# Up projection of a hybrid decoder layer: seven products for eight (Strassen-Winograd), gated activations kept in DRAM, one down projection over all 22 channel tiles

## The chip, the cores and the metric

The kernel runs on one core of a Trainium2 chip. The metric is the device time of one execution in microseconds (us). The kernel before takes 1457.86 us (median of 3 runs, 1457.52 to 1457.88). The changed kernel is to be compared with it on the same chip.

The engines are named as in the profile: PE (TensorE, matmuls and transposes), PEld (the loads of the stationary operand, which lie beside PE), DVE (VectorE), ACT (ScalarE), POOL (GpSimd) and SP (SyncE, which here only issues DMAs).

## The reference, cut to what matters

One layer, 1024 tokens of width 1024, float32:

```python
u = rms_norm(h) @ w_in
oA = gated_delta_net(u[...])          # 4 heads
oB = diff_attention(u[...])           # 4 heads
h = h + concat(oA, oB) @ w_out
g, v = split(causal_dwconv3(rms_norm(h) @ w_up))   # 2 x 2816 channels, 3 taps and a bias
h = h + (silu(g) * v) @ w_down
```

The change touches only the last two lines and the second norm ahead of them (and where one set of buffers of `w_out` lies).

## The kernel before

**Arithmetic.** Every large matmul is done in three: an operand is split into a high part (an ACT copy, L196) and the remainder (a subtraction on DVE, L200, or POOL, L198), and hi·hi, hi·lo and lo·hi are summed in PSUM. A matmul has a stationary operand of 128x128 and a moving one of 128x512.

**Attention and output projection.** After delta rule and attention, `wout_b` goes through eight blocks of 128 tokens, from the last to the first: transposes of the mixed heads (`trm`), the product with the second half of `w_out` (`pwo`, two halves of 512 columns), residual, second norm (`u2`), and eight transposes (`tr`), which `split_T` turns into the high and low parts of the normed activations `x2n`, channels on partitions (ACT L251, DVE L252).

**Up projection.** `ffn_up(j)` makes channel tile j of the gate and tile 22+j of the other half. Each is [128 channels, 1024 tokens] in PSUM: `gemm_T` (matmuls L416, L417, L418) runs over 8 row blocks of `w_up`, 3 matmuls each, for both halves of 512 tokens: 48 matmuls a tile, 96 for a pair, 22 pairs. Tile j's weight is one load of 128 columns (512 KB) and one split of 1024 elements. The convolution over tokens reads PSUM: an ACT Identity with the last tap and the bias (L1169), two fused multiply-adds on DVE (L1172), then Silu on ACT (L1175) for the gate, and the product of the two on POOL (L1177).

**Down projection.** The products stay in SBUF, twelve tiles in the first run of `ffn_down`, ten in the second, since there is room for no more. Each run splits them (L1199 on ACT, L1200 on DVE), multiplies by `w_down` (`mm3`, L377 to L379, eight PSUM banks at once, one for each token block, for one half of the 1024 output columns at a time), adds the residual (L1222) and writes to DRAM: the first run to `h2_dram`, the second, which reads `h2_dram` as its residual, to the output.

**What sets the order.** A tile framework schedules each engine's instructions by priorities (the table `PRI`) and by the order of the code, and puts semaphores between them. Buffers come from rings: `g` (16 of 128x1024), `w` (5, split weights), `raw` (3, weights as loaded), `c` (4), `l` (2), `j` (2), `xn` (4 of 128x4096, the normed activations). A new tile takes the slot of an old one of its ring and waits for the last reader of that. SP's queue issues DMAs in order, and one that waits for a slot holds those behind it. In `before` the first pair's matmuls stand between those of `wout_b`'s last blocks, since they need the later half of the tokens alone.

## Time and profile before

| | |
|---|---|
| median of 3 runs | 1457.86 us |
| profiled execution, span from first to last instruction | 1450.8 us |
| mean granted TensorE clock | 0.988 of full |
| PE busy | 1382.0 us (95%), 8191 matmuls |
| DVE, ACT, POOL busy | 753.7, 530.8, 255.4 us (52%, 37%, 18%) |
| DMA | 128.9 MB |

The profiled execution's own time lies in its span; the median of the runs is 7.06 us above the span. A row of the slices below gives the busy tenths of 40 stretches of 36.3 us. PE has 9s from the 21st slice (about 725 us) to the 39th: that is the feed-forward part, with the up and down projections, and DVE, ACT and POOL have 3s, 2s and 0s or 1s there.

```text
PE   7988898989979999999999999999999999999998
DVE  6457978885343477867753333333333333333343
ACT  6435454532333456574332222222221222222221
POOL 3144312140342253430001011010000011010000
```

In the groups of instructions "mean ns of one" of a matmul is the time of one from start to modelled end, and matmuls overlap; how often one can start is read from the number that start in a window in which PE was never idle.

### The profile page before, as it was taken

Reading aid. Unit: us, or ns where it says so; the run is one execution under the profiler, and the core shown is the slowest. Engines: PE = TensorE matmul, PEld = TensorE weight load, DVE = VectorE, ACT = ScalarE, POOL = GpSimd, SP = SyncE. Lnnn points to the kernel's source line nnn. Section 1 sums busy time; section 2 is a strip of 40 time slices with the busy share of each in tenths; the row PEclk is TensorE's granted clock in tenths of the full one; section 3 lists DMA queues with packets and bytes.
Section 4 is the critical chain, followed back from the end, with each engine's and each line's share of the span. In section 5 each row is a group of like instructions: output and inputs, shape, how many; then the busy total and the mean of one; then the engine's idle time right before and its main releaser. Section 6 shows DMA issues by size and latency. Waiting matters only on the chain.

```text
span 1450.8 us, 20362 instructions
## 1 busy us (share of the span) xinstructions
PE 1382.0 (95%) x8191; PEld 1166.8 (80%) x8191; DVE 753.7 (52%) x1579; ACT 530.8 (37%) x970; POOL 255.4 (18%) x199
## 2 busy tenths in 40 slices
PE   7988898989979999999999999999999999999998
PEld 7877677878979977777788888888888888888887
DVE  6457978885343477867753333333333333333343
ACT  6435454532333456574332222222221222222221
POOL 3144312140342253430001011010000011010000
PEclk8999999999999999999999999999999999999999
DMA  7321112121732467554321111113234111112231
GB/s 226 85 72 44 31 30 73 59 75 59 206 100 88 117 165 176 130 166 151 127 74 58 44 45 57 44 45 116 76 98 136 53 44 59 44 44 81 79 116 58
DMA packets 136221, 128.90 MB, mean 89 GB/s; under 512 B 8255, under 2 KB 111295, under 8 KB 136127
## 3 DMA queue, kind: packets, MB, share of 16 engines
q1 hardware_dynamic: 123647, 117.92, 26.1%
q0 software_dynamic: 11008, 8.39, 3.1%
q10 hardware_dynamic: 1472, 1.29, 0.3%
q8 instruction: 64, 1.05, 0.3%
q14 instruction: 30, 0.25, 0.1%
HBM read 92.44 MB, written 30.95 MB: 85 GB/s over the span
## 4 chain that ended last, share of the span: by engine, by line
PE 75%; DVE 11%; issue 5%; POOL 3%; ACT 3%; DMA 3%; SPq 0%; DVEq 0%; ACTq 0%; POOLq 0%
PE gT L418 12%; PE gT L417 12%; PE gT L416 12%; PE pd L377 6%; PE pd L379 6%; PE pd L378 5%; PE pn L397 4%; PE pn L398 3%; PE pn L400 3%; DVE acc L567 2%; PE pT L872 1%; DMA raw<-in_w_in_dram 1%; PE pwo L377 1%; PE pwo L379 1%; PE pao L930 1%
## 5 line engine op out<-in xcount | busy, mean ns | idle before, releaser
L416 PE MATMUL gT<-xn,whi 128*128 128x512 f32 x896 | 352.4, 393 | 0.8 <-ACT pT L427 0.8
L418 PE MATMUL gT<-xn,wlo 128*128 128x512 f32 x896 | 352.8, 394 | 0.0
L417 PE MATMUL gT<-xn,whi 128*128 128x512 f32 x896 | 351.8, 393 | 0.0
L200 DVE TENSOR_TENSOR wlo<-raw,whi 128x1024 fp32r<-128x1024 f32 x66 | 80.9, 1225 | 331.6 <-PE gT L417 266.5
L416 PEld LDWEIGHTS gT<-xn,whi 128*128 128x128 f32 x896 | 168.8, 188 | 34.7 <-ACT pT L427 1.2
L417 PEld LDWEIGHTS gT<-xn,whi 128*128 128x128 f32 x896 | 168.8, 188 | 34.0
L418 PEld LDWEIGHTS gT<-xn,wlo 128*128 128x128 f32 x896 | 169.0, 189 | 33.7
L1177 POOL TENSOR_TENSOR facc<-facc,facc 128x1024 f32<-128x1024 f32 x22 | 52.6, 2392 | 647.0 <-DVE facc L1172 608.2
L1169 ACT ACTIVATE facc<-gT,fcw 128x1024 f32<-128x1024 f32 x44 | 53.3, 1211 | 291.7 <-PE gT L418 291.7
L377 PE MATMUL pd<-whi,gh 128*128 128x512 f32 x352 | 137.5, 391 | 0.0
L378 PE MATMUL pd<-wlo,gh 128*128 128x512 f32 x352 | 137.0, 389 | 0.0
L379 PE MATMUL pd<-whi,gl 128*128 128x512 f32 x352 | 136.8, 390 | 0.0
L196 ACT ACTIVATE whi<-raw 128x1024 fp32r<-128x1024 f32 x100 | 105.1, 1051 | 48.9 <-PE pd L379 28.0
L1172 DVE SCALAR_TENSOR_TENSOR facc<-gT,fcw,facc 128x1023 f32<-128x1023 f32 x88 | 112.9, 1282 | 11.6 <-ACT facc L1169 10.1
L198 POOL TENSOR_TENSOR wlo<-raw,whi 128x1024 fp32r<-128x1024 f32 x34 | 83.7, 2471 | 191.4 <-PE gT L418 66.7
L397 PE MATMUL pn<-whi,xn 128*128 128x256 f32 x448 | 114.8, 290 | 0.0
L398 PE MATMUL pn<-whi,xn 128*128 128x256 f32 x448 | 114.2, 289 | 0.0
L1199 ACT ACTIVATE gh<-facc 128x1024 fp32r<-128x1024 f32 x40 | 42.5, 1061 | 159.8 <-PE pd L378 125.5
L1200 DVE TENSOR_TENSOR gl<-facc,gh 128x1024 fp32r<-128x1024 f32 x40 | 48.9, 1223 | 91.0 <-ACT gh L1199 91.0
L397 PEld LDWEIGHTS pn<-whi,xn 128*128 128x128 f32 x448 | 86.0, 192 | 0.4
L398 PEld LDWEIGHTS pn<-whi,xn 128*128 128x128 f32 x448 | 85.9, 192 | 0.1
L377 PEld LDWEIGHTS pd<-whi,gh 128*128 128x128 f32 x352 | 66.1, 188 | 15.1 <-ACT gh L1199 1.0
(304 smaller groups left out, 2219.6 us busy)
## 6 DMA issues: line engine op xcount, KB each, us to landing
raw<-in_w_up_dram SPq DMA_DIRECT2D x44, 512.0 KB, 3.8
raw<-in_w_down_dram SPq DMA_DIRECT2D x22, 512.0 KB, 3.8
raw<-in_w_in_dram SPq DMA_DIRECT2D x18, 512.0 KB, 4.0
pn_dram<-pn SPq DMA_DIRECT2D x16, 512.0 KB, 3.5
fres<-h_dram SPq DMA_DIRECT2D x16, 512.0 KB, 4.9
raw<-in_w_in_dram SPq DMA_DIRECT2D x17, 256.0 KB, 3.7
x<-in_x_dram SPq DMA_DIRECT2D x8, 512.0 KB, 5.8
qk<-pn_dram SPq DMA_DIRECT2D x8, 512.0 KB, 3.5
```

The costliest lines, as they stand in the source:

```text
L196: S.activation(hi, raw[:, 0:w], AF.Copy)
L198: G.tensor_tensor(lo, raw[:, 0:w], hi.bitcast(F32), op=ALU.subtract)
L200: V.tensor_tensor(lo, raw[:, 0:w], hi.bitcast(F32), op=ALU.subtract)
L377: PE.matmul(ps, lh, rh, start=first, stop=False)
L378: PE.matmul(ps, lh, rl, start=False, stop=False)
L379: PE.matmul(ps, ll, rh, start=False, stop=last)
L397: PE.matmul(o, xs(xn, 0, kt, a, b), wh, start=kt == 0, stop=False)
L398: PE.matmul(o, xs(xn, 1, kt, a, b), wh, start=False, stop=False)
L416: PE.matmul(o, whi[:, kt, :], xs(x_, 0, kt, *qs), start=kt == 0, stop=False)
L417: PE.matmul(o, whi[:, kt, :], xs(x_, 1, kt, *qs), start=False, stop=False)
L418: PE.matmul(o, wlo[:, kt, :], xs(x_, 0, kt, *qs), start=False, stop=kt == NK - 1)
L1172: V.scalar_tensor_tensor(acc[:, sft:], ps[:, :T - sft], fcw[:, jj * 44 + ct:jj * 44 + ct + 1], acc[:, sft:], op0=ALU.mult, op1=ALU.add)
```

## The change

The gate tile j and the up tile 22+j are taken together as a matrix product of 2x2 blocks: the weight rows in two halves of four row blocks, the two channel tiles, the tokens in two halves of 512. Seven products of 12 matmuls (4 row blocks by 3) replace eight. The sums that this takes:

- On the activations, in `combine` instead of `split_T`, token block by token block: T1, T2, T3, T4 are sums of the first and second halves of tokens and channels. The token halves "11", "21", "22" and T2 are split at once; T1, T3 and T4 are kept as sums and split by `mv_split` at the start of the feed-forward part (24 ACT, 16 DVE and 8 POOL instructions of 128x256).
- On the weights, for each j: four sums of 128x512 on POOL (L1269 to L1272), and splits of three tiles of 1024 and one of 512 where there were two of 1024.
- On the results, for each j: six DVE adds of 128x512 from PSUM to SBUF (L1280) and two ACT copies (L1288, L1297). The convolution (L1307, L1310) then reads SBUF.

`up_early` does the two products that need the later half of the tokens alone, for j = 0 and 1, before the transposes of the last token blocks. The eight PSUM banks become tiles of 512. `up` writes each product of gate and up tile to `act_dram`; `down` runs once over 22 tiles, loads them back (for both column halves, 42 loads in all, since the last pair is kept), splits them and adds the residual once (16 adds rather than 32). The second-half `w_out` splits move from ring `g` to `w`, `l` and `j`.

The core of the diff:

```diff
-            split_T(norm_T(u, sm), x2n, tt)
+            combine(norm_T(u, sm), u, tt)
...
+    def combine(pss, u, tt):
+        o = slice(tt % 4 * P, tt % 4 * P + P)
+        by = lambda ap: ap.rearrange("p (k t) -> p k t", t=P)
...
+        if tt >= 4:
...
+            for q, name in enumerate(("11", "21")):
+                hv, lv = (t[:, :, o] for t in stage[name])
+                S.activation(hv, by(pss[q]), AF.Copy)
+                V.tensor_tensor(lv, by(pss[q]), hv.bitcast(F32), op=ALU.subtract)
+                S.activation(stage[tt][q][:, half], pss[q], AF.Copy)
+            return
...
+        S.activation(t3, b12, AF.Copy)
+        V.tensor_tensor(t1, b12, t1, op=ALU.subtract)
+        V.tensor_tensor(t2, b22, t1, op=ALU.subtract)
+        V.tensor_tensor(t3, b22, t3, op=ALU.subtract)
...
+        S.activation(hv, by(t2), AF.Copy)
+        G.tensor_tensor(lv, by(t2), hv.bitcast(F32), op=ALU.subtract)
+        G.tensor_tensor(t4, t4, t2, op=ALU.subtract)
...
+    def product(ps, w, name, start):
+        wh, wl = w
+        xh, xl = mv[name]
+        for k in range(4):
+            ks = slice(k * P, (k + 1) * P)
+            first = start and k == 0
+            PE.matmul(ps, wh[:, ks], xh[k], start=first, stop=False, skip_group_check=not start)
+            PE.matmul(ps, wh[:, ks], xl[k], start=False, stop=False, skip_group_check=not start)
+            PE.matmul(ps, wl[:, ks], xh[k], start=False, stop=k == 3, skip_group_check=not start)
...
+        G.tensor_tensor(s1, a21, a22, op=ALU.add)
+        G.tensor_tensor(s2, s1, a11, op=ALU.subtract)
+        G.tensor_tensor(s3, a11, a21, op=ALU.subtract)
+        G.tensor_tensor(s4, a12, s2, op=ALU.subtract)
+        ws2, w11 = halves(split_w(x_))
+        ws1, ws3 = halves(split_w(y_))
+        w12, ws4 = halves(split_w(z_, None, T, jtr))
...
+        product(a, ws2, "T2", True)
...
+            product(e, w11, "11", True)
+            S.activation(x1, e, AF.Copy)
...
+        product(c, ws1, "T1", True)
+        add(cg[:, FIRST], a, x1)
+        product(a, ws3, "T3", False)
+        add(cu[:, FIRST], c, x1)
...
+            product(e, w12, "21", False)
+            S.activation(cg[:, LAST], e, AF.Copy)
+        add(cu[:, FIRST], a, cu[:, FIRST])
+        product(c, ws4, "22", False)
+        add(cg[:, FIRST], c, cg[:, FIRST])
+        product(a, w22, "T4", False)
+        add(cu[:, LAST], a, x1)
...
+        nc.sync.dma_start(act_dram[j * P:(j + 1) * P, :], accs[1])
...
+                        g_ = ct_("act")
+                        nc.sync.dma_start(g_, act_dram[i * P:(i + 1) * P, :])
+                        gh, gl = gtr("gh"), gtr("gl")
...
-    ffn_down(g0 + [ffn_up(j) for j in range(1, 12)], 0, h_dram, h2_dram)
-    ffn_down([ffn_up(j) for j in range(12, NF)], 12, h2_dram, out2)
+    for j in range(NF):
+        up(j, early[j] if j < EARLY else None)
+    down()
```

How the order moves, at three places. First PE at the end of `wout_b`. Before, where `gT` is the first channel tile's product and `pwo` the output projection:

```order
2956 L418 MATMUL gT_7828<-xn_7286,wlo_7832 128x512
2957 L378 MATMUL pwo_7697<-wlo_6715,mhl_7694 128x512
2958 L416 MATMUL gT_7828<-xn_7286,whi_7831 128x512
2959 L379 MATMUL pwo_7697<-whi_6714,mhl_7694 128x512
2960 L417 MATMUL gT_7828<-xn_7287,whi_7831 128x512
2961 L377 MATMUL pwo_7697<-whi_6714,mhl_7694 128x512
```

PE in the changed kernel at that place, where `pe` is the first early product:

```order
2991 L383 MATMUL pwo_7729<-whi_6732,mhl_7712 128x512
2992 L384 MATMUL pwo_7729<-wlo_6733,mhl_7712 128x512
2993 L385 MATMUL pwo_7729<-whi_6732,mhl_7712 128x512
2994 L246 MATMUL tr_7797<-k_sb,u_1273_7780 128x128 x4
2995 L246 MATMUL tr_7802<-k_sb,u_1273_7780 128x128 x4
2996 L1230 MATMUL pe_7870<-x_1162_7294,whi_7865 128x512
```

The feed-forward matmuls that stood between those of `pwo` now stand behind all of them. POOL at the same time, before: the last splits of `w_out`, then nothing until the first gate product.

```order
133 L198 TENSOR_TENSOR wlo_6715<-raw_6712,whi_6714 128x1024
134 L198 TENSOR_TENSOR wlo_6721<-raw_6718,whi_6720 128x1024
135 L198 TENSOR_TENSOR wlo_6727<-raw_6724,whi_6726 128x1024
136 L198 TENSOR_TENSOR wlo_6733<-raw_6730,whi_6732 128x1024
137 L1177 TENSOR_TENSOR facc_7943<-facc_7883,facc_7943 128x1024
```

POOL in the changed kernel: the weight sums of j = 0 and j = 1 (`rx`, `ry`, `rz` hold weights), one copy, and only then the two instructions that finish T4 and T2 (`xT_1257` is the low part of T2) for the last token block.

```order
145 L1269 TENSOR_TENSOR ry_7993<-rw_7995 128x512
146 L1271 TENSOR_TENSOR ry_7993<-rx_7992,rw_7995 128x512
147 L1270 TENSOR_TENSOR rx_7992<-ry_7993,rx_7992 128x512
148 L1290 COPY cg_8018<-early_7869 128x512
149 L1272 TENSOR_TENSOR rz_7994<-rz_7994,rx_7992 128x512
150 L1269 TENSOR_TENSOR ry_8100<-rw_8102 128x512
151 L1271 TENSOR_TENSOR ry_8100<-rx_8099,rw_8102 128x512
152 L1270 TENSOR_TENSOR rx_8099<-ry_8100,rx_8099 128x512
153 L1272 TENSOR_TENSOR rz_8101<-rz_8101,rx_8099 128x512
154 L1105 TENSOR_TENSOR k_1218_7518<-k_1218_7518,u_1282_7817 128x512
155 L1104 TENSOR_TENSOR xT_1257_7692<-u_1282_7817,xT_1257_7692 128x4x128
```

Eleven instructions of 128x512 now stand in a row ahead of the first full product. Second place, DVE in the steady up projection. Before, two multiply-adds and one weight split for each channel tile:

```order
1282 L1172 SCALAR_TENSOR_TENSOR facc_9143<-gT_9088,fcw,facc_9143 128x1023
1283 L1172 SCALAR_TENSOR_TENSOR facc_9143<-gT_9088,fcw,facc_9143 128x1022
1284 L200 TENSOR_TENSOR wlo_9275<-raw_9272,whi_9274 128x1024
1285 L1172 SCALAR_TENSOR_TENSOR facc_9203<-gT_9148,fcw,facc_9203 128x1023
1286 L1172 SCALAR_TENSOR_TENSOR facc_9203<-gT_9148,fcw,facc_9203 128x1022
```

DVE in the changed kernel, most of one period (one j), which repeats; `pa` and `pc` are PSUM banks, `cg` and `cu` the results of gate and up tile, `rx`, `ry`, `rz`, `rw` the weights of the next j:

```order
1436 L1280 TENSOR_TENSOR cu_9962<-pc_9964,cu_9962 128x512
1437 L206 TENSOR_TENSOR wlo_10080<-rx_10068,whi_10079 128x1024
1438 L206 TENSOR_TENSOR wlo_10084<-ry_10069,whi_10083 128x1024
1439 L1280 TENSOR_TENSOR cu_9962<-pa_9963,cu_9962 128x512
1440 L1280 TENSOR_TENSOR cg_9961<-pc_9964,cg_9961 128x512
1441 L206 TENSOR_TENSOR wlo_10088<-rz_10070,whi_10087 128x1024
1442 L1310 SCALAR_TENSOR_TENSOR acc_10057<-cg_9961,fcw,acc_10057 128x1023
1443 L1280 TENSOR_TENSOR cu_9962<-pa_9963,cu_9962 128x512
1444 L1310 SCALAR_TENSOR_TENSOR acc_10057<-cg_9961,fcw,acc_10057 128x1022
1445 L1279 TENSOR_TENSOR w_1608_10091<-rw_10071,w_1608_10091 128x512
1446 L1310 SCALAR_TENSOR_TENSOR acc_10062<-cu_9962,fcw,acc_10062 128x1023
1447 L1310 SCALAR_TENSOR_TENSOR acc_10062<-cu_9962,fcw,acc_10062 128x1022
```

The splits of the next weights now stand among the adds that free PSUM. Third place, SP where the up projection ends. Before, with the activations in SBUF, only weights are loaded:

```order
222 L208 DMA raw_11141<-in_w_up_dram 128x8x128
223 L208 DMA raw_11201<-in_w_up_dram 128x8x128
224 L1190 DMA raw_11264<-in_w_down_dram 128x2x512
225 L1190 DMA raw_11326<-in_w_down_dram 128x2x512
226 L1190 DMA raw_11388<-in_w_down_dram 128x2x512
```

SP in the changed kernel there:

```order
243 L1327 DMA raw_11072<-in_w_down_dram 128x2x512
244 L1327 DMA raw_11138<-in_w_down_dram 128x2x512
245 L1358 DMA fres_11606<-h_dram 128x2x512
246 L1336 DMA act_10880<-act_dram 128x1024
247 L1336 DMA act_10886<-act_dram 128x1024
248 L1316 DMA act_dram<-acc_10860 128x1024
```

The first two loads of activations stand right ahead of the write of the last activation tile; they go into slots of the ring `c`, which the last `up` uses for `cg`, `cu` and the two accumulators.

## Rows read from the trace of the kernel before

**Rows 1.** The cores' view: span and mean granted clock.

```profile
core 0: 1450.8 us, clock 0.988
```

**Rows 2.** Windows; columns: stretch, length, busy us (instructions) by engine, clock, DMA.

```profile
1000.00:1100.00 100.00, 100.00 (x441) 82.41 (x441) 36.02 (x34) 26.32 (x26) 0.00 (x0) 1.00 0.25 81
1100.00:1200.00 100.00, 100.00 (x442) 82.44 (x441) 38.86 (x35) 25.32 (x24) 7.17 (x3) 1.00 0.27 83
1200.00:1300.00 100.00, 100.00 (x442) 82.79 (x442) 34.12 (x27) 23.91 (x23) 11.95 (x5) 1.00 0.17 48
```

**Rows 3.** Costliest groups: line, engine, operation, operands, count | busy us, mean ns.

```profile
L416 PE MATMUL gT<-xn,whi 128*128 128x512 f32 x896 | 352.4, 393 | 0.8 <-ACT pT L427 0.8
L200 DVE TENSOR_TENSOR wlo<-raw,whi 128x1024 fp32r<-128x1024 f32 x66 | 80.9, 1225 | 331.6 <-PE gT L417 266.5
L1177 POOL TENSOR_TENSOR facc<-facc,facc 128x1024 f32<-128x1024 f32 x22 | 52.6, 2392 | 647.0 <-DVE facc L1172 608.2
L1169 ACT ACTIVATE facc<-gT,fcw 128x1024 f32<-128x1024 f32 x44 | 53.3, 1211 | 291.7 <-PE gT L418 291.7
L196 ACT ACTIVATE whi<-raw 128x1024 fp32r<-128x1024 f32 x100 | 105.1, 1051 | 48.9 <-PE pd L379 28.0
```

**Rows 4.** Groups kept apart by shape, of DVE, ACT and POOL.

```profile
L1172 DVE SCALAR_TENSOR_TENSOR facc<-gT,fcw,facc 128x1023 f32<-128x1023 f32 x44 | 56.4, 1283 | 10.1 <-ACT facc L1169 10.1
L1222 DVE TENSOR_TENSOR fres<-pd,fres 128x512 f32<-128x512 f32 x32 | 20.6, 685 | 16.3 <-PE pd L379 16.3
L251 ACT ACTIVATE xn<-tr 128x512 fp32r<-128x512 f32 x32 | 17.7, 592 | 25.9 <-PE tr L240 25.7
L313 POOL TENSOR_TENSOR w<-raw,w 128x512 fp32r<-128x512 f32 x1 | 1.3, 1272 | 0.0
L840 POOL TENSOR_TENSOR qk<-qk,qkw 128x512 f32<-128x512 f32 x16 | 21.9, 1390 | 58.2 <-issue 45.6 <-DVE qk L837 8.2 <-ACT pn L403 4.4
```

**Rows 5.** Timeline of DVE, three stretches: start, length, line, operands, count.

```profile
98.74 10.22 DVE L567 SCALAR_TENSOR_TENSOR acc<-pT,dcw,acc 128x1023 f32<-128x1023 f32 x6
...
420.59 2.47 DVE L850 TENSOR_TENSOR sqk<-qk,sn 128x128 f32<-128x128 f32 x1 [2.73 <-POOL qk L840]
...
635.80 0.69 DVE L1038 TENSOR_TENSOR xa<-pwo,xa 128x512 f32<-128x512 f32 x1 [1.42 <-PE pwo L379]
```

**Rows 6.** Timeline of POOL in the same stretches.

```profile
100.95 3.35 POOL L198 TENSOR_TENSOR wlo<-raw,whi 128x1024 fp32r<-128x1024 f32 x1
...
420.52 4.74 POOL L198 TENSOR_TENSOR wlo<-raw,whi 128x1024 fp32r<-128x1024 f32 x2
...
632.37 7.05 POOL L198 TENSOR_TENSOR wlo<-raw,whi 128x1024 fp32r<-128x1024 f32 x3 [13.80 <-ACT whi L196]
```

**Rows 7.** Line 850: count, then shortest, median, longest ns.

```profile
L850 DVE TENSOR_TENSOR sqk<-qk,sn x8: 275/292/2474, 401.4 to 611.4; 128x128 f32<-128x128 f32 x8
```

**Rows 8.** Windows of line 416 alone, PE and PEld, at the feed-forward start.

```profile
690.00:752.70 62.70, 15.60 (x39) 7.33 (x40) 1.00 0.34 115
```

**Rows 9.** Timeline of PE, the last output-projection matmul, and of DVE, two adds in a row.

```profile
729.14 0.40 PE L379 MATMUL pwo<-whi,mhl 128*128 128x512 f32 x1
...
1446.29 1.29 DVE L1222 TENSOR_TENSOR fres<-pd,fres 128x512 f32<-128x512 f32 x2 [1.43 <-PE pd L379]
```

**Rows 10.** DMA issues: median us to landing.

```profile
fres<-h_dram SPq DMA_DIRECT2D x16, 512.0 KB, 4.9
raw<-in_w_up_dram SPq DMA_DIRECT2D x44, 512.0 KB, 3.8
qk<-pn_dram SPq DMA_DIRECT2D x8, 512.0 KB, 3.5
```

**Rows 11.** Windows after stretches in which PE was partly idle.

```profile
110.00:120.00 10.00, 9.75 (x48) 8.27 (x49) 3.03 (x12) 7.08 (x37) 0.11 (x1) 0.74 0.00 0
430.00:440.00 10.00, 10.00 (x71) 9.28 (x70) 4.68 (x11) 7.00 (x20) 2.14 (x4) 0.87 0.44 122
```

More of the change, by code (lines that the diff above doesn't have):

```diff
@@ L31 @@
 GB, WB, RB, LB, JB, CB, SB, OB, LA, S1, S2 = 16, 5, 3, 2, 2, 4, 8, 1, 2, 3, 5
+EARLY = 2
 WARM = 15
@@ L39 @@
 PP0, PP1 = 4, 2
-Q1 = 2
 PRE_K = {5: 1, 6: 0}
@@ L1057, in wout_b @@
         nc.scalar.dma_start(w2row, norm2_w.broadcast_to([P, D]))
-        wfs = [load_wo(4, c, G, gtr) for c in range(2)]
+        spare = itertools.chain([wt] * 5, [ltr] * 2, [jtr])
+        wfs = [load_wo(4, c, G, lambda s: next(spare)(s)) for c in range(2)]
         def tile_(tt):
@@ L1149, in hybrid_layer, with bank @@
     pctx.close()
-    pf = [ctx.enter_context(tc.tile_pool(name=f"pf{i}", bufs=2, space=bass.MemoryType.PSUM, reuse_waits="tile"))
+    pf = [ctx.enter_context(tc.tile_pool(name=f"pf{i}", bufs=4, space=bass.MemoryType.PSUM, reuse_waits="tile"))
           for i in range(2)]
-    turn = itertools.count()
-    def big(s="big"):
-        return pf[1 - next(turn) // 2 % 2].tile([P, T], F32, tag="big", name=nm(s))
-    def ffn_up(j):
-        accs = []
-        for part in range(2):
-            ct = part * NF + j
-            ps = big("gT")
-            for _ in gemm_T(wup, ct * P, x2n, lambda q: ps[:, q * 512:(q + 1) * 512], None,
-                            (1, 0) if j < Q1 else (0, 1)):
-                pass
-            acc = gt("facc")
-            S.activation(acc, ps, AF.Identity, scale=fcw[:, 88 + ct:89 + ct], bias=fcw[:, 132 + ct:133 + ct])
+    def bank(i, s):
+        return pf[i % 2].tile([P, 512], F32, tag="b", name=nm(s))
@@ new lines, in hybrid_layer, with mv_split @@
+    act_dram = dp.tile([FFN, T], F32, name="act_dram")
+    def mv_split(name, src, lo_eng):
+        tiles = [[gtr("x" + name) for _ in range(2)] for _ in range(2)]
+        mv[name] = [[tiles[p][k // 2][:, k % 2 * 512:k % 2 * 512 + 512] for k in range(4)] for p in range(2)]
+        for tt in (3, 2, 1, 0):
+            sv = src(tt).rearrange("p (k t) -> p k t", t=P)
+            for i in range(2):
+                hv, lv = (tiles[p][i].rearrange("p (k t) -> p k t", t=512)[:, :, tt * P:tt * P + P] for p in range(2))
+                S.activation(hv, sv[:, 2 * i:2 * i + 2], AF.Copy)
+                lo_eng.tensor_tensor(lv, sv[:, 2 * i:2 * i + 2], hv.bitcast(F32), op=ALU.subtract)
@@ new lines, in raw_, with halves, up_early @@
+    def raw_(s="raw"):
+        return rp.tile([P, T], F32, tag="raw", name=nm(s))
+    def halves(hl):
+        return [tuple(t[:, i * 512:(i + 1) * 512] for t in hl) for i in range(2)]
+    LAST, FIRST = slice(512, 1024), slice(0, 512)
+    def up_early(j):
+        e_raw = raw_()
+        G.tensor_copy(e_raw[:, 0:1], o3[1][:, 0:1])
+        load_half(e_raw, 0, j * P, 8)
+        w11, w12 = halves(split_w(e_raw, None, T, gtr))
+        kept = gt("early")
+        e = bank(1, "pe")
+        product(e, w11, "11", True)
+        S.activation(kept[:, 0:512], e, AF.Copy)
+        product(e, w12, "21", False)
+        S.activation(kept[:, 512:1024], e, AF.Copy)
+        return kept
@@ L1177, in ffn_up, with down @@
         G.tensor_tensor(accs[1], accs[0], accs[1], op=ALU.mult)
-        return accs[1]
-    def ffn_down(gs, k0, src, dst):
-        pairs = [(i, i + 1) for i in range(0, len(gs), 2)]
+        nc.sync.dma_start(act_dram[j * P:(j + 1) * P, :], accs[1])
+    def down():
+        pairs = [(i, i + 1) for i in range(0, NF, 2)]
         kept = None
```

87 lines of the change are left out of this document (71 added, 16 removed).

## The prediction

> **What bounds the kernel now.** I read the cores' view first, for the span, then the slices of the page, then windows of the last half, then the groups, and only then single rows. The span is 1450.8 us [rows 1]. From the 21st slice on PE is never idle, and DVE, ACT and POOL are busy for a third of the time or less: in three windows of 100 us each PE is busy for all 100 us at the full granted clock, and 441 to 442 matmuls start in each [rows 2]. So the feed-forward part is bound by the number of its matmuls, one every 100/441.5 = 0.2265 us. The 393 ns of the groups [rows 3] is the latency of one, with its neighbours lying over it, and must not be used as the price: 264 matmuls would seem worth 104 us by it and are worth 264 x 0.2265 = 59.8 us. Every idle microsecond of PE that the change brings into this part counts in full against that.
>
> **1. Matmuls removed: -59.8 us.** 84 instead of 96 for each of 22 pairs is 264 fewer, of the same shape. The down projection keeps its 1056. The pace is that of windows with PE always busy, so the sum holds only where the other engines keep up; the next four parts ask for that.
>
> **2. The steady period (one j).** PE needs 84 x 0.2265 = 19.03 us. Beside it lie, by the nearest rows, four POOL sums at 1.27 and one product at 2.39 (7.5 us), 3.5 splits at 1.23, six adds at 0.69 and four multiply-adds at 1.28 on DVE (13.5 us), some 8.6 us on ACT [rows 3, 4]. None is a bound by its sum. But the order makes a loop through three engines, from the end of product "22" of one j to the start of product "T4" of the next, which is seven products, 19.03 us, later: ACT splits z (1.05), DVE its low part (1.23), multiply-add (1.28), add (0.69), multiply-add (1.28), low part of w22 (0.69), two multiply-adds (2.57), POOL the product (2.39) and three sums (3.82), ACT the high part of x (1.05), DVE two low parts (2.46) and one add (0.69): 19.2 us by the means. Seven of the DVE steps do not depend on the one before and run into it: two adds end within 1.29 us, not 1.37 [rows 9], so 7 x 0.08 = 0.6 comes off; the passes from engine to engine put about 0.4 back by my estimate. POOL's fourth sum then still runs when the low part of x is due. Whether that matters, the trace shows: an instruction of DVE with two SBUF operands took 2.47 us beside a POOL subtraction where its median is 0.29 [rows 5 to 7], whereas one that reads PSUM and SBUF took 0.69 beside the same POOL line, its usual time. So the low part waits out the rest of the sum, 1.27 - 1.05 = 0.2 us, and the loop is 19.2 us. Since a wait ahead of T4 delays the next "22" too, a loop of C costs w = (C - 19.03)/2 in each period: 0.1 us, 20 periods, **+2 us**. Lower end 0 (C under 19.03). Upper end: sums at 1.39 [rows 4] and multiply-adds, which now read SBUF twice, at 10.22/6 = 1.70, as six of them took beside POOL [rows 5, 6], make C = 19.2 + 0.36 + 1.7 = 21.3, w = 1.1, 22 us. I stay by the low end since in this loop POOL starts only after the multiply-adds have ended.
>
> [...]
>
> **3. The start of the feed-forward part.** Before, 3 x 39 = 117 of its matmuls had started by 752.7 us [rows 8], many between those of the output projection, whose last one starts at 729.14 [rows 9]. In the changed order none stands ahead of the last `pwo`. Those then end earlier, by my estimate at 725. The path from there: residual add 0.69, square and the high part of the first early weight on ACT (2 x 1.05), 12 matmuls (2.7), copy 0.59, high and low part of the second early weight (1.05 + 1.23), which ends near 734; its release lets POOL begin the first weight sum. POOL then has eleven instructions of 128x512 in a row (the order shows them), 11 x 1.27 = 14.0 us, and between the fifth and the sixth a wait for ACT and DVE to split y of j = 0, two high parts and one low part after the last sum, 1.05 + 1.05 + 1.23 = 3.3. The low part of T2 is the last of the eleven: 734 + 17.3 + 0.5 for passes = 752. PE has by then done the 48 early matmuls and waits twice, some 4.5 us behind copies that stand behind ACT's weight splits, and some 3 us for T2. 117 - 48 = 69 matmuls behind at about equal time: 69 x 0.2265 = **+15.6 us**. Lower end 8 (the output projection, freed of foreign matmuls, ends at its earliest: 27 to 33 of them at 0.2265 is 6 to 7.5 us). Upper end 22: three low parts of DVE meet sums of POOL and wait for one each, and the eleven run at 1.39.
>
> **4. The first three j.** POOL has eight small splits of T4 after the eleven (about half a sum each, 5 us) before it can sum the weights of j = 2, so the loop of part 2 starts late. The 120 matmuls of j = 0 and 1 (27 us) cover most: I take **+3 us** (1 to 6), an estimate from the same durations.
>
> **5. From up to down.** Before, activations lie in SBUF and PE goes through without a gap. Now the first down matmul needs activation tile 0 back from DRAM, in a slot of ring `c` that is free only after the last multiply-add on the last gate tile. From the start of the last product: add 0.69, Identity 1.21, multiply-add 1.28, add 0.69, multiply-add 1.28, passes 0.2: 5.35 us. The load: 3.5 to 4.9 us for 512 KB [rows 10], 4.5 with the issue; high part 1.05, pass 0.1. That is 11.0 after the start of a product of 2.72 us: PE idle for 8.3 us, and 0.8 more for the low part (1.23 against two matmuls that need it not). [...] Together 9.1 + 2.2 = **+11.3 us** (7 to 14). The further loads run ahead of use, since ring `c` is then theirs alone and a pair of tiles lasts PE 48 x 0.2265 = 10.9 us.
>
> **6. At nothing.** The halved residual work and the missing `h2_dram`: they lay beside busy PE (32 adds of 0.69) [rows 4]. The added DRAM traffic: the DMA share is 0.17 to 0.27 in the windows [rows 2], and a tile of 512 KB in each 19 us is little. The moved `w_out` splits: the order of everything before about 640 us is the same, 0 ± 3.
>
> **The sum.** -59.8 + 2 + 15.6 + 3 + 11.3 = -27.9. The profiled execution's span becomes 1450.8 - 27.9 = 1422.9 us. The median of the runs lies 7.06 us above the span (1457.86 - 1450.8); I keep that: **1430 us**.
>
> **Rivals.**
> - *Cheap borders.* If POOL begins its sums as soon as their weights land, and the load of tile 0 lands at 3.5 us, parts 3 to 5 come to 8 + 1 + 7 and the loop to 0: -43.8, 1414 us. For it: weights are loaded long ahead. Against it: the first sum waits, by the order, for the slot of an early weight.
> - *The loop binds.* C = 20.3 (sums at 1.39, two of four multiply-adds at 1.70): w = 0.65, 13 us in place of 2: 1441 us. For it: the margin is 1% of the period, which is less than the spread of the means. Against: it needs two engines to meet that the loop keeps apart.
> - *Slower than before.* The multiply-adds and splits of DVE and the sums of POOL meet in every period, because a delay once shifts one against the other: four multiply-adds at 1.70 (+1.7), the product at 3.35 instead of 2.39 (+0.96), three sums longer by the same ratio, 1.4 (+1.5) [rows 5, 6]. C = 23.4, w = 2.2, 44 us in place of 2: about 1472 us. It decides from w = 1.5, C = 22. For it: the rows show both sides stretched at once. Against: POOL's product needs the last multiply-add, and the splits need the sums, so that they cannot lie beside each other without breaking a dependence. [...]
> - *Priced by latency.* 104 us in place of 59.8 would give about 1386. I give it 1 in 100: the number of starts in the windows excludes it.
>
> **How the numbers follow.** The forecast, 1422 to 1437, has 0.50; cheap borders, 1405 to 1422, 0.18; the loop that binds, 1437 to 1455, 0.23; slower, 0.08; the last 0.01. The range from 1413 to 1447 leaves out about 0.08 below and 0.12 above. A difference within 0.2% (2.9 us) can't be told from no change here; of the third case some 0.03 lies there. Faster 0.88, same 0.04, slower 0.08.
>
> **What would show it.** In the changed profile: windows of 100 us in the up projection in which PE is busy for 99 or more and still starts about 441 matmuls (parts 1, 2); the first T2 matmul at 752 ± 5 us with PE idle for some 7 us ahead of it (3); one gap of PE of 8 to 10 us between the up and down projections, ended by the ACT split of a loaded activation, and a clock below 1 behind it (5); multiply-adds at 1.28 and POOL sums at 1.27. I am wrong in part 2 if PE's idle time recurs in each period ahead of T4, in part 3 if T2 starts ten microseconds off, and altogether if the window counts fall, since then the saved matmuls don't turn into time.

## The result: faster by half a per cent, a third of the forecast gain

The changed kernel took 1448.47 us (median of 11 runs, 1445.1 to 1452.94) against 1457.86 us for the kernel before (11 runs): ratio 0.9945, 95% interval 0.993 to 0.996. The sign is the one forecast. The size is not: 9.4 us saved instead of 28, and 1448.47 lies above the range's upper end of 1447.

The page after, to be set beside the span and clock of [rows 1]: PE now 93% busy with 264 matmuls fewer, the granted clock a little lower.

```profile
core 0: 1444.5 us, clock 0.972
PE 1340.6 (93%) x7927; PEld 1128.8 (78%) x7927; DVE 886.0 (61%) x1745; ACT 612.0 (42%) x1098; POOL 388.2 (27%) x307
PEclk8999999999999999999998999999999998999999
```

The last line is the clock of 40 slices. Apart from the first, two slices of it are not full: the 22nd, from 758 us on (start of the up projection), and the 34th, from 1192 on (start of the down projection). The profiled span was forecast at 1422.9 and is 1444.5, so 21.6 us are to be found. Four marks on PE divide it into five stretches; the forecast of the last one is what the others leave of 1422.9:

| stretch | forecast us | measured us | difference |
|---|---|---|---|
| start to last `pwo` | 725.0 | 737.45 | +12.4 |
| last `pwo` to first T2 matmul | 27 | 31.56 | +4.6 |
| T2 to last up matmul (1800 matmuls) | 407.7 + 2 + 3 | 420.58 | +7.9 |
| last up to first down matmul | 8.5 | 7.43 | -1.1 |
| first down matmul to end | 249.7 | 247.48 | -2.2 |

The marks are these rows of PE (start, length, operands, idle time ahead and its releaser):

```profile
737.45 0.39 PE L385 MATMUL pwo<-whi,mhl 128*128 128x512 f32 x1
769.01 0.77 PE L1230 MATMUL pa<-xT,whi 128*128 128x512 f32 x1 [4.80 <-DVE x L1101]
1189.59 0.39 PE L1232 MATMUL pa<-xT,w 128*128 128x512 f32 x1
1197.02 0.80 PE L383 MATMUL pd<-whi,gh 128*128 128x512 f32 x1 [7.05 <-ACT gh L1338]
```

The rest of the difference, from 21.6 to the 18.5 us between 1430 and 1448.47, is that the median lies 4.0 us above the profiled span here and not 7.06 as before. Each run is only 1.7 us longer than its own span (the profiled one took 1446.19 us), so most of the 7.06 that the forecast carried over was the place of one execution among the runs, and no constant.

**The steady loop.** Windows of 100 us in the up projection, columns as in [rows 2]: PE busy for all of it, full clock, and as many matmuls as before.

```profile
850.00:950.00 100.00, 100.00 (x442) 82.35 (x441) 62.93 (x66) 41.81 (x46) 41.67 (x30) 1.00 0.26 85
1000.00:1100.00 100.00, 99.98 (x441) 82.21 (x440) 64.03 (x68) 41.97 (x46) 41.03 (x28) 1.00 0.26 85
```

So the 264 removed matmuls are worth their 59.8 us, and everything lost is lost at the borders of the loop. The head of the list of PE's waits from 640 us on says where (instruction waited for, us in all, times, longest):

```profile
PE pd L383 <- ACT gh L1338: 7.0, 1, 7.0
PE pa L1230 <- DVE x L1101: 4.8, 1, 4.8
PE pe L1230 <- ACT early L1255: 4.4, 2, 3.7
PE pa L1230 <- DVE cg L1280: 4.3, 2, 2.5
```

The first three of these were forecast (8.3, "some 3" and "some 4.5"). The fourth was not, nor was the price of a wait beyond its own length anywhere but in part 5. The next rows show that price.

**After the long waits the matmuls start 0.43 us apart.** PE around T2, rows in order:

```profile
758.82 0.80 PE L1230 MATMUL pe<-x,whi 128*128 128x512 f32 x1 [3.74 <-ACT early L1255]
759.41 0.63 PE L1231 MATMUL pe<-x,whi 128*128 128x512 f32 x1
...
773.41 0.63 PE L1231 MATMUL pa<-xT,whi 128*128 128x512 f32 x1
773.84 0.57 PE L1232 MATMUL pa<-xT,wlo 128*128 128x512 f32 x1
774.24 0.39 PE L1230 MATMUL pc<-xT,whi 128*128 128x512 f32 x1
774.47 0.40 PE L1231 MATMUL pc<-xT,whi 128*128 128x512 f32 x1
```

A row of the length 0.63 is followed by the next start after 0.43, one of 0.39 after 0.23. The granted clock is 0.50 of full from 758.80 to 763.50 and from 769.10 to 773.80, and 1.00 from 774.30 to 779.00. Two whole products of twelve, the last early one and T2, run at the lower level and lose 12 x 0.2 = 2.4 us each.

### The profile page after: what moved, and what is told of

It reads as the page before. It is cut to its first block, busy times and chain, and to the rows that moved or that the text cites. A ratio compares the mean times of both kernels' runs of the same rounds, so it can differ in the third digit from the quotient of the medians.

```text
span 1444.5 us, 20625 instructions
## 1 busy us (share of the span) xinstructions
PE 1340.6 (93%) x7927; PEld 1128.8 (78%) x7927; DVE 886.0 (61%) x1745; ACT 612.0 (42%) x1098; POOL 388.2 (27%) x307
## 3 DMA queue, kind: packets, MB, share of 16 engines
q10 hardware_dynamic: 1472, 1.29, 0.3%
## 5 line engine op out<-in xcount | busy, mean ns | idle before, releaser
L1315 POOL TENSOR_TENSOR acc<-acc,acc 128x1024 f32<-128x1024 f32 x22 | 53.5, 2432 | 241.6 <-issue 196.6
L1338 ACT ACTIVATE gh<-act 128x1024 fp32r<-128x1024 f32 x42 | 44.4, 1060 | 134.6 <-PE pd L384 113.8
L1339 DVE TENSOR_TENSOR gl<-act,gh 128x1024 fp32r<-128x1024 f32 x42 | 51.8, 1237 | 67.8 <-ACT gh L1338 67.6
L202 ACT ACTIVATE whi<-raw 128x1024 fp32r<-128x1024 f32 x58 | 61.0, 1052 | 50.8 <-issue 18.3
L1230 PE MATMUL pa<-xT,whi 128*128 128x512 f32 x176 | 71.2, 404 | 9.2 <-DVE x L1101 4.8
L424 PE MATMUL gT<-xn,wlo 128*128 128x512 f32 x192 | 78.7, 410 | 0.0
L385 PEld LDWEIGHTS pd<-whi,gl 128*128 128x128 f32 x352 | 66.7, 190 | 15.2 <-DVE gl L1339 1.4
L422 PE MATMUL gT<-xn,whi 128*128 128x512 f32 x192 | 78.2, 407 | 0.0
L206 DVE TENSOR_TENSOR wlo<-raw,whi 128x1024 fp32r<-128x1024 f32 x24 | 30.1, 1254 | 78.3 <-PE pd L384 57.9
L423 PE MATMUL gT<-xn,whi 128*128 128x512 f32 x192 | 77.7, 405 | 0.0
L384 PEld LDWEIGHTS pd<-wlo,gh 128*128 128x128 f32 x352 | 66.8, 190 | 14.0
L1230 PE MATMUL pe<-x,whi 128*128 128x512 f32 x176 | 70.6, 401 | 5.5 <-ACT early L1255 4.4
```

The source lines that it names most:

```text
L202: S.activation(hi, raw[:, 0:w], AF.Copy)
L206: V.tensor_tensor(lo, raw[:, 0:w], hi.bitcast(F32), op=ALU.subtract)
L384: PE.matmul(ps, lh, rl, start=False, stop=False)
L385: PE.matmul(ps, ll, rh, start=False, stop=last)
L422: PE.matmul(o, whi[:, kt, :], xs(x_, 0, kt, *qs), start=kt == 0, stop=False)
L423: PE.matmul(o, whi[:, kt, :], xs(x_, 1, kt, *qs), start=False, stop=False)
```

## The experiments

The stretch up to about 616 us, which the change leaves in its order, ended anywhere from 614.7 to 623.8 us in the profiles. So times within a profile are counted from the issue of the last four loads of K on POOL (616.41 us in the kernel before, 616.67 in the changed one). "Control" is the changed kernel again, run in the third batch. Ratios are to the kernel before on the same chip; before's median was 1454.96, 1453.91 and 1454.03 us in the batches of runs 1 to 4, 5 to 8, and 9 to 12.

| run | last `pwo` | T2 | last up | first down | end | median us | ratio (95%) |
|---|---|---|---|---|---|---|---|
| before | 112.7 | | | | 834.4 | 1457.86 | 1 |
| changed | 120.8 | 152.3 | 572.9 | 580.4 | 827.8 | 1448.47 | 0.9945 (0.993 to 0.996) |
| e1 half on DVE | 116.5 | 148.4 | 569.2 | 576.6 | 824.2 | 1445.80 | 0.993 (0.991 to 0.995) |
| e2 other slot | 122.0 | 153.6 | 576.4 | 576.7 | 820.0 | 1439.14 | 0.9895 (0.987 to 0.992) |
| e3 T2 first | 121.7 | 151.4 | 571.0 | 578.5 | 825.9 | 1445.51 | 0.9936 (0.991 to 0.996) |
| e4 rings | 119.0 | 136.3 | 568.0 | 575.3 | 822.0 | 1442.78 | 0.9912 (0.989 to 0.994) |
| e5 no early | 121.6 | 145.7 | 576.9 | 584.2 | 830.8 | 1450.38 | 0.9964 (0.994 to 0.998) |
| e6 no copies | 118.2 | 150.6 | 570.2 | 577.6 | 823.9 | 1445.75 (one run) | |
| e7 combination | 117.9 | 149.9 | 574.5 | 574.7 | 818.1 | 1438.68 | 0.9879 (0.986 to 0.990) |
| e8 e7, no early | 118.4 | 142.6 | 576.8 | 577.0 | 820.5 | 1442.96 | 0.9913 (0.989 to 0.994) |
| e9 fillers | 120.8 | 159.0 | 575.3 | 582.6 | 829.0 | 1451.96 | 0.9977 (0.996 to 0.999) |
| e10 late loads | 116.4 | 148.3 | 571.3 | 571.5 | 814.9 | 1433.05 | 0.986 (0.983 to 0.989) |
| e11 rings, late loads | 120.6 | 137.9 | 570.4 | 570.6 | 814.4 | 1433.26 | 0.9848 (0.982 to 0.988) |
| control | 121.0 | 152.5 | 573.0 | 580.3 | 827.9 | 1446.47 | 0.9939 (0.992 to 0.996) |

The control repeats the marks of the changed kernel to 0.2 us, but runs whose engines have the same order up to a mark can differ there by more: the last `pwo` comes at 120.8 to 122.0 in the changed kernel, the control, e2 and e9, at 116.4 to 117.9 in e1, e7 and e10, at 119.0 and 120.6 in e4 and e11. So a difference of less than some 2 us between two single columns is not read as an effect.

### e1: half of the moved splits on DVE

```
-        wfs = [load_wo(4, c, G, lambda s: next(spare)(s)) for c in range(2)]
+        wfs = [load_wo(4, c, (G, V)[c], lambda s: next(spare)(s)) for c in range(2)]
```

> Two of the four low parts of w_out's second half go from POOL to DVE. Theory A (the moved splits delay the output projection: in the changed kernel POOL makes four of them in 10.00 us from 645.13, PE is busy for 4.69 of 10 us behind that, and the last pwo matmul starts at 737.45 instead of 729.14): the four are done some 5 us earlier, the last pwo moves ahead by 4 to 6 us and the time falls by 4 to 7 us from 1448.5, the clock that no longer falls included. Rival B (the output projection is late because each of its blocks takes longer with combine than with split_T: the eight trm groups follow each other in 9.0 us on average instead of 8.0): the last pwo moves by less than 2 us and the time by less than 2 us.

POOL splits the second half of `w_out`; in the kernel before three of the four were done by 639.4 [rows 6]. POOL in the changed kernel:

```profile
645.13 10.00 POOL L204 TENSOR_TENSOR wlo<-raw,whi 128x1024 fp32r<-128x1024 f32 x4 [26.31 <-PE pwo L384]
```

The first of the four waits for a `pwo` of the last block of `wout_a`, whose weights hold the slots that the new ones now share, and the others follow in one piece. PE then stands for half of one window, where the kernel before had PE busy for 9.61 us of the same ten:

```profile
650.00:660.00 10.00, 4.69 (x34) 3.78 (x32) 8.27 (x15) 3.72 (x9) 5.13 (x2) 0.91 0.27 94
```

POOL in e1:

```profile
643.18 4.79 POOL L204 TENSOR_TENSOR wlo<-raw,whi 128x1024 fp32r<-128x1024 f32 x2 [26.30 <-PE pwo L384]
```

The last `pwo` comes 4.3 us earlier, T2 3.9, the end 3.6; e7 and e10, with the same edit, have the last `pwo` at 117.9 and 116.4. The late splits are shown as the cause of some 4 us at the last `pwo`, half of the 8.1 by which it is later than before.

How they cost it is read from the changed kernel's trace. PE does not wait for their results: the last one ends at 655.13, and the first `pwo` that uses them starts at 665.69. But DVE, which does the softmax of the attention at that time, is held up beside them:

```profile
645.41 2.17 DVE L917 SCALAR_TENSOR_TENSOR sums<-sums,nlam 128x1 f32<-128x1 f32 x1
647.62 2.98 DVE L919 SCALAR_TENSOR_TENSOR p<-p,sums,p 128x640 f32<-128x640 f32 x1
...
652.76 0.68 DVE L1044 TENSOR_TENSOR xa<-pwo,xa 128x512 f32<-128x512 f32 x1
...
659.71 0.58 PE L903 MATMUL S<-K,Q 128*128 128x256 f32 x1 [3.51 <-ACT p L913]
665.69 0.40 PE L383 MATMUL pwo<-whi,mhl 128*128 128x512 f32 x1
```

The same lines took 0.21 and 0.88 us in the kernel before, and two more instructions of a single column took 2.07 and 1.79 us here: four instructions with two SBUF operands, 7.5 us lost, while one that reads PSUM and SBUF kept its 0.68. The last row but one ends a wait of PE for ACT, which had waited 4.85 us for DVE's maxima. In e1 two of the four are stretched. Since e1 also changes the order of PE from about 655 us on, the share of this stretching in its 4 us is argued and not measured.

### e2: the first two loaded activations in slots that are free early

```
-                        g_ = ct_("act")
+                        g_ = raw_("act") if c == 0 and pr is order[0] else ct_("act")
```

> The first two activation tiles of the down projection are loaded into slots of the ring of raw weights, which are free from about 1165 us on, instead of ring c, which is free only after the last multiply-adds. Theory A (PE idles for 7.0 us between up and down only for that load, and loses some 2.6 us more to the lower clock behind it): the wait on the ACT split of the activation goes, the first down matmul follows the last up matmul within 1 us, and the time falls by 8 to 10 us from 1448.5. Rival B (the second pair's activations, still in ring c, are late in their turn, since a pair lasts PE 10.9 us): only 1 to 4 us are won and a new wait of PE on ACT stands one pair later.

PE in e2 goes from up to down without a gap, and at full pace:

```profile
1197.69 0.39 PE L1232 MATMUL pa<-xT,w 128*128 128x512 f32 x1
1197.92 0.39 PE L383 MATMUL pd<-whi,gh 128*128 128x512 f32 x1
```

From the last up matmul to the end the trace has 243.6 us instead of 254.9: the slot of ring `c` costs 11.3 us. Some 2 us come back as a wait of 2.5 us shortly ahead of it, of a `pe` matmul for ACT's copy `cu`: the splits of the early loads now come ahead of that copy in ACT's order (e10 tests this).

### e3: T2 ahead of the weight sums of j = 1 on POOL

```
+        if j == 1:
+            G.tensor_copy(y_[:, 0:1], mv["T2"][1][3][:, 0:1].bitcast(F32))
         G.tensor_tensor(s1, a21, a22, op=ALU.add)
```

> A copy of one column makes POOL's first weight sum of j = 1 wait for the low part of T2, so that three of the four sums of j = 1 stand behind T2 and T4 of the last token block instead of ahead of them. Theory A (the first full product waits for POOL's row of eleven instructions): T2 of j = 0 starts 3 to 4 us earlier than 769.0, and the time falls by 2 to 4 us, as the sums of j = 1 are needed only 13.6 us later. Rival B (it is DVE that ends the wait, the low part of the last '22' block behind T1's splits): the start moves by less than 1 us, and the time by less than 1 us. Rival C: the sums of j = 1 are then late themselves and PE waits ahead of j = 1: no gain or a loss of up to 3 us.

The copy makes the first sum of j = 1 wait for T2. T2's first matmul moved by 0.9 us only, or by 1.8 counted from the last `pwo`, and its wait ends on DVE all the same. In the changed kernel the forecast's chain of eleven POOL instructions ran as forecast (18.3 us from its first to T2, forecast 18), but it is not alone in setting T2. DVE beside it, in the changed kernel:

```profile
761.90 0.67 DVE L1098 TENSOR_TENSOR t<-tr,t 128x512 f32<-128x512 f32 x1
762.50 5.76 DVE L1220 TENSOR_TENSOR xT<-k,xT 128x256 fp32r<-128x256 f32 x4
768.19 0.68 DVE L1101 TENSOR_TENSOR x<-tr,x 128x512 fp32r<-128x512 f32 x1
768.79 1.08 DVE L1220 TENSOR_TENSOR xT<-k,xT 128x256 fp32r<-128x256 f32 x3
```

While POOL sums, a split of T1 takes 5.76/4 = 1.44 us; once POOL is idle, 1.08/3 = 0.36. This is the meeting of two SBUF operands with POOL that part 2 of the prediction weighed and kept out of the loop; it came in the start.

In e3 the four splits take 2.34 us together, but then POOL's last instruction for T2 and DVE both wait for ACT:

```profile
767.07 0.60 ACT L1257 ACTIVATE early<-pe 128x512 f32<-128x512 f32 x1 [2.96 <-PE pe L1232]
768.26 1.27 POOL L1104 TENSOR_TENSOR xT<-u,xT 128x512 fp32r<-128x512 f32 x1 [2.49 <-ACT xT L1103]
768.71 0.69 DVE L1101 TENSOR_TENSOR x<-tr,x 128x512 fp32r<-128x512 f32 x1 [1.65 <-ACT x L1100]
```

ACT's two high parts (L1103, L1100) stand behind its copy of the last early product, which waits for PE. So with POOL out of the way the early products themselves hold T2 back, which e5 measures.

### e4: the two rings exchanged

```
-        wfs = [load_wo(4, c, G, lambda s: next(spare)(s)) for c in range(2)]
+        wfs = [load_wo(4, c, G, gtr) for c in range(2)]
...
-        w11, w12 = halves(split_w(e_raw, None, T, gtr))
+        w11, w12 = halves(split_w(e_raw))
```

> The rings are exchanged: w_out's second half is split into ring g, as in the kernel before, and the early weights into ring w, so that neither waits for the first half of w_out or for the slots of wout_b's rows. In the built order the early products now stand between the last blocks of the output projection. Theory A (what the forecast got wrong is the start: slots make the w_out splits and the early products late): the last pwo at 725 to 732, the first T2 at 750 to 756 instead of 769.0, and the time falls by 12 to 18 us. Rival B (the longer blocks of combine set the pace): T2 starts at 760 or later, and the time falls by less than 8 us.

T2 starts 16 us earlier and the up projection ends only 4.9 us earlier. PE's waits in e4:

```profile
PE pa L1229 <- DVE cg L1279: 10.4, 3, 6.0
PE tr L246 <- DVE u L276: 8.3, 6, 3.3
...
PE pa L1229 <- ACT xT L1103: 5.2, 1, 5.2
```

Waits for DVE have grown from 4.3 to 10.4 and from 3.6 to 8.3. From 710 to 760 us DVE is busy for 47.9 of 50 us there, against 37.9 in the changed kernel. So of the 16 us that T2 gains 11 are given back, 6.0 of them in one wait for DVE's `cg`: DVE's adds, splits and rows of the last token blocks bind the start about as much as the POOL chain that the prediction followed.

### e5 and e8: no early products

```
-EARLY = 2
+EARLY = 0
```

> The changed kernel without early products: all of j = 0 and 1 waits for the last token block. In the built order POOL's weight sums of j = 0 then stand ahead of T2 and T4 of the last two blocks, because their slots in the ring of raw weights are no longer held by the early weights. Theory A (in the changed kernel the start is bound by the chain through ACT, DVE and POOL, which the early products lengthen; the 48 early matmuls run at half clock and between waits): T2 of j = 0 starts 8 to 12 us earlier after the last pwo matmul than the 31.6 us of the changed kernel, the 48 matmuls (10.9 us) come after it, and the time changes by less than 3 us either way. Rival B (the early products hide 10.9 us of matmuls in time that is idle anyhow): the time rises by 6 to 11 us.

T2 starts 24.1 us behind the last `pwo` instead of 31.6, with 48 matmuls still to do, which are worth 10.9 us. So the early products delay T2 by 7.4 us and save 3.5; the end is 3.0 us later without them, 2.2 counted from the last `pwo`. They gain, though less than a third of their matmuls' worth. In e8 (the edit of e7 below with no early products) the end is 2.4 us later than in e7, 2.0 counted from the last `pwo`.

> The same three edits without early products. By theory A of the run without early products it is within 3 us of the run with the three edits, by its rival 6 to 11 us slower than that.

### e6: without the copies of the later token half

```
+                for t in stage[tt]:
+                    G.memset(t, 0.0)
...
-                S.activation(stage[tt][q][:, half], pss[q], AF.Copy)
```

> combine leaves out the plain copies of the later token half (two ACT copies of 128x512 in each of the first four blocks); T1 and T4 are then sums with zeros, and the output is not the reference's. Theory A (each block of the output projection is slower because combine puts more on ACT and DVE than split_T): the first four steps from one trm group to the next fall from some 8.3 us to 7.3 us as before the change, and the last pwo comes 3 to 4 us earlier. Rival B (the blocks are slower for another reason, the late w_out splits or the loads): the steps stay at 8.2 us or more.

This run leaves out the copies of the later token half, whose quadrants are zero instead. The question was why the blocks of `wout_b` are longer: from the second block's `trm` to the last one's it is 48.7 us before and 55.1 after. PE waits 6.8 us in that stretch where it waited 2.5: for DVE's `u` 3.6 instead of 1.6, for ACT's `mhl` 1.9 and `p` 1.3 instead of nothing. The granted clock is 0.97 of it instead of 1.00, which is another 1.7 us.

Without the copies the stretch is 54.8 us, but that does not rule them out, since the edit also changes the order of PE from 686 us on. Up to the sixth block's `trm` it is 32.9 us, where the changed kernel has 34.8 and the kernel before 31.1; then one step of 13.6 us follows where the changed kernel has 8.4. The last `pwo` comes 2.6 us earlier. So the copies, or the order that goes with them, are at most 1.9 of the 3.7 us in the first of these stretches, and what makes up the rest is open. In the second and third block the attention output `pao` stands ahead of the next `trm` in PE's order in the changed kernel and behind it in the kernel before. Whether that is a cause was not tried.

### e7: e1, e2 and two `w_down` splits on POOL

```
-                wh, wl = (... for t in split_w(raw))
+                wh, wl = (... for t in split_w(raw, G if c == 0 and pr[0] < 4 else None))
```

> Three edits together: half of the low parts of w_out's second half on DVE, the first two activation tiles in the ring of raw weights, and the low parts of the first two w_down tiles on POOL instead of DVE. If the causes are separate and add, 4 us from the first and 7.5 us from the second as measured alone; the third should take the 2.5 us wait of PE on the DVE add near the end of the last up products and the 1.5 us of lower clock behind it: 12 to 16 us less than the changed kernel, about 1433. If the third only moves the wait to ACT or POOL: 10 to 12 us less.

The end comes 9.7 us earlier, where e1 and e2 gave 3.6 and 7.8. The wait that e2 had made grew:

```profile
PE pe L1230 <- ACT cu L1288: 4.2, 1, 4.2
```

### e9: filler matmuls behind the last early product

```
+    def warm_mm(n, w):
+        d = bank(0, "pw")
+        for i in range(n):
+            PE.matmul(d, w[0][:, 0:P], mv["11"][0][0], start=True, stop=True)
...
+        if j == 1:
+            warm_mm(18, w11)
```

> 18 matmuls of 128x512 whose result nobody reads are put behind the last early product, where PE waits 4.8 us for T2 in the changed kernel and then makes the first 12 matmuls of T2 at half clock (0.43 us apart instead of 0.2265). Theory A (each wait is paid twice, once as idle time and once as half clock behind it): PE stays busy, the 12 matmuls of T2 come 0.2265 us apart, 2.4 us are won, and nothing is lost as the wait was there anyhow: from the start of T2 to the end of the up projection 2 to 3 us less. Rival B (the clock falls here for another reason than the wait): T2 still at half clock, and the time the same or up to 2 us longer.

The fillers were to run in the wait ahead of T2. They did not: they took over the wait itself and ran behind it.

```profile
774.17 6.80 PE L1249 MATMUL pw<-x,whi 128*128 128x512 f32 x18 [4.78 <-DVE x L1101]
780.81 0.40 PE L1230 MATMUL pa<-xT,whi 128*128 128x512 f32 x1
781.05 0.39 PE L1231 MATMUL pa<-xT,whi 128*128 128x512 f32 x1
```

So T2 was 6.7 us later, and the run cannot say what filling the wait is worth. It says what the wait is for. The fillers read only the half "11" and an early weight, both long in use, and still they wait 4.78 us for the DVE instruction that T2 waits for in the changed kernel (4.80). What they share with T2 is a new PSUM bank of the same pool (`bank(0, ...)`), and the DVE instruction, L1101, reads the transposes `tr` of the last rows out of PSUM. So the wait ahead of T2 is read as one for a PSUM bank. L1101 ends at 768.87 (e3 has its row), T2's own low part on POOL at 767.98:

```profile
766.54 1.44 POOL L1104 TENSOR_TENSOR xT<-u,xT 128x512 fp32r<-128x512 f32 x1
```

No run moved the bank. The run also shows the clock: behind 6.8 us of matmuls T2 starts at 0.23 us apart, and from T2 to the next wait for `cg` there are 38.7 us against 41.3 in the changed kernel. The lower clock costs 2.6 us there, close to the 2.4 of the rows. (The profiled span is 5.8 us above the control's: 1.1 of it behind 616 us, by the marks, and 4.7 ahead of it, not explained.)

### e10 and e11: late loads, and the rings again

Both add this to e2's edit and e7's splits; e10 has e1's edit beside it, e11 e4's.

```
+        last[j] = accs[1]
...
+                        if c == 0 and pr is order[0]:
+                            G.tensor_copy(g_[:, 0:1], last[NF - 2][:, 0:1])
                         nc.sync.dma_start(g_, act_dram[i * P:(i + 1) * P, :])
```

> As the run with three edits, but the two early activation loads wait for POOL's product of j = 20, so that their splits stand behind the last copies of the up products on ACT. Theory A (the new wait of 4.2 us of PE on ACT's copy in that run comes from the two splits that stand ahead of it): the wait goes, and the time is 4 to 6 us below that run, at a ratio of 0.984 to 0.986 to the kernel before. Rival B (the copy is late for the splits of w_down): the wait stays above 3 us.

> The end of the run before this one together with the exchanged rings (w_out's second half in ring g, the early weights in ring w), in place of the low parts on DVE. By the two measured apart: 5 to 6 us from the rings and 10 to 13 us from the end, a ratio of 0.982 to 0.986 to the kernel before. Rival: as in the run with exchanged rings, what is won ahead of T2 is lost in waits for DVE in j = 0 to 2, and the ratio is that of the run before this one or higher.

The copy holds the first loads back until POOL has made the product of the last tile but one, so that ACT's splits of them come behind its copy `cu`. That wait is gone; a wait for DVE's `cg` stands in its place, in e10:

```profile
1173.20 0.80 PE L1230 MATMUL pa<-xT,whi 128*128 128x512 f32 x1 [3.78 <-DVE cg L1282]
```

Both end some 13 us ahead of the changed kernel and are 1.4 and 1.5% faster than the kernel before. Their intervals lie below those of both kernels, and which of the two is faster they do not tell.

The control, with what was expected of it:

> The changed kernel unaltered, beside the others on the same chip, to see by how much two measurements of one kernel differ: a ratio of 0.993 to 0.996 to the kernel before, as in the first comparison.

Its median is 2.0 us from that of the first runs.

## Why the prediction was wrong, point by point

**Right: the price of a matmul (part 1).** 441 to 442 in 100 us, before and after.

**Right on the loop (part 2).** +2 us forecast, about 0 found: PE idles for 0.02 us in the window from 1000 to 1100. (The 1.70 us for a multiply-add, in the upper end and in two rivals, was a mean of six beside POOL; line by line four of the six took 1.27 or 1.28 us and two took 2.12 and 3.40.) The means of its links held: multiply-adds 1.28, sums 1.29 to 1.34, product 2.43.

```profile
L1315 POOL TENSOR_TENSOR acc<-acc,acc 128x1024 f32<-128x1024 f32 x22 | 53.5, 2432 | 241.6 <-issue 196.6 <-DVE acc L1310 30.1 <-ACT whi L202 14.9
L1272 POOL TENSOR_TENSOR rz<-rz,rx 128x512 f32<-128x512 f32 x22 | 29.5, 1342 | 1.6
L1310 DVE SCALAR_TENSOR_TENSOR acc<-cu,fcw,acc 128x1023 f32<-128x1023 f32 (+1 forms) x44 | 56.7, 1288 | 0.9
```

**Right: up to down (part 5).** 11.3 us forecast; 11.3 by e2. Of it 7.05 are the wait (8.3 forecast), 0.65 that for the low part (0.8), and the rest the lower clock: 3.4 found, as 243.4 us from the first down matmul to the end in e2 against 247.5, with a granted clock of 0.50 from 1197.10 to 1203.00. The sum has 2.2 there, a term that no run shows; the windows of [rows 11], with mean clocks of 0.74 and 0.87, lie in other stretches. The mechanism is right; that the sum is right to the tenth is luck, since two terms are off by 1.2 in opposite directions.

**Wrong: "the moved `w_out` splits: the order of everything before about 640 us is the same, 0 ± 3" (part 6).** This step failed most. The order is the same, but the slots are not: the splits take slots that `wout_a`'s weights hold until its last block, and come in one piece of 10.00 us, beside which four DVE instructions with two SBUF operands took 7.5 us longer than the same lines before, and PE is busy for 4.69 of the 10 us from 650 on. e1 shows 4 us of it. The rows of POOL [rows 6] showed when the splits had run before; what I left out was who holds their new slots at that time, and what DVE does then.

**Wrong: "Those then end earlier, by my estimate at 725" (part 3).** The last `pwo` is at 737.45, 8.3 later than before instead of 4 earlier: 4 from the splits, and the blocks themselves are 6.4 us longer (of which 2 come back at the end). I priced the removal of matmuls from a stretch that had few of them: 24 stood ahead of the last `pwo`, where I had counted 27 to 33, and all but one of the 24 in the last block. The blocks ahead of it had none to lose. PE's waits for ACT and DVE between them grew by 4.3 us; ACT, with `combine` in place of `split_T`, is busy for 25.1 us there instead of 20.0, DVE for 38.2 instead of 37.9. Which part of that work binds stays open (e6).

**Wrong in size: the start (part 3).** From the last `pwo` to T2 it is 4.6 us more than forecast, though POOL's chain took its 18 us. What the chain starts from came late: 13.2 us behind the last `pwo` instead of 9. In between stand the transposes of the last rows, which the forecast did not list, a split of DVE that took 1.93 us beside POOL instead of 1.23, and seven matmuls at the lower clock (743.75 to 746.90, 3.15 us instead of 1.59, granted clock 0.50). And the chain is not what T2 waits for last: that is, as e9 is read, a PSUM bank, freed by DVE 0.9 us after the chain's end. e3 and e4 show that shortening POOL alone gains little, since DVE and ACT are late next.

**Wrong in size: the first and the last j (part 4).** Beyond the 407.7 us of its 1800 matmuls the stretch holds 12.9 us, where parts 2 and 4 had 5. Windows of PE (busy, clock), where a full one counts 46 because it also counts those that reach over its edges:

```profile
769.00:779.00 10.00, 9.99 (x33) 0.74 0.09 27
...
799.00:809.00 10.00, 8.78 (x37) 1.00 0.36 105
809.00:819.00 10.00, 8.72 (x31) 0.83 0.13 53
...
1169.00:1179.00 10.00, 7.50 (x31) 0.90 0.31 107
1179.00:1189.00 10.00, 10.00 (x43) 0.93 0.53 157
```

Missing are 13, 24 and 18 matmuls, 12.5 us at 0.2265: T2 at the lower clock, and two waits for `cg` with the lower clock behind each. (The lower clock behind these two came again in the control, but not in every run; the last section has the rows.) At the end of the up projection DVE splits the first tile of `w_down` ahead of the add that frees the bank:

```profile
1175.58 1.22 DVE L206 TENSOR_TENSOR wlo<-raw,whi 128x1024 fp32r<-128x1024 f32 x1
1176.71 0.68 DVE L1280 TENSOR_TENSOR cg<-pa,cu 128x512 f32<-128x512 f32 x1
```

That the next phase's first splits fall into the last period of the loop was in no part of the prediction. No rival describes what came: the loop that binds (1441) and the meeting of DVE and POOL in every period (1472) are excluded by the windows, cheap borders (1414) by the waits. The time came out 7 us above the first of these, and for another reason.

## What to carry to other kernels

When matmuls are taken out, price them by starts per window, then walk the borders of the phase: which slot, or PSUM bank, each moved load, split or product waits for and who holds it, what DVE does beside a POOL instruction that moves, and what the next phase puts into the orders of ACT and DVE during the last period. A wait of PE cost more than its length in the changed kernel: the matmuls that start at the lower clock cost 1.5 to 3.4 us behind waits of 1.4 to 7 us, though behind the one of 1.77 us nine other runs lost only 0.1. Where one engine's chain binds a start, look at how busy the others are there before shortening it; of 16 us taken from T2's start in e4, 11 were lost again.
